# A two-layer hybrid encoder trunk: low weight halves of the mixers moved to GpSimd, index search dealt out in steps, reciprocals merged, feed-forward begun by two outputs

## The chip, the cores and the metric

The kernel runs on one core of one Trainium2 chip. The metric is device time in microseconds (us) of one execution; lower is better. The kernel before takes 1246.18 us (median of 3 runs, 1245.75 to 1247.45).

## The reference

A trunk of two layers over x of 512 frames by 1024 channels, float32. Each layer is RMSNorm, a mixer with residual, RMSNorm, and a gated feed-forward block with residual; a last RMSNorm ends it. Cut to what matters:

```python
# layer 0 mixer
qa, ka, va, qi, ki, wi, qb, kb, vb = _split(xn @ w_in, EVEN_SPLITS)
score = einsum('bqhs,bqh->bqs', relu(qi . ki), wi)      # index scores, masked by chunk
idx = top_k(score, 128)                                 # A: 8 heads, softmax over the 128 chosen keys
ya = softmax(qa . ka[idx] * scale) @ va[idx]
yb = softmax(qb . kb * scale + rel_bias) @ vb           # B: 8 heads, learned distance bias
y  = concat(ya, yb) @ w_out
# layer 1 mixer
F  = cumsum(log_sigmoid(fc + forget_b))                 # C: 8 heads, bias F[t] - F[s], causal
yc = softmax(qc . kc * scale + F[t] - F[s]) @ vc
yd = softmax_with_sink(qd . kd * scale, window) @ vd    # D: 8 heads on 2 key heads
y  = concat(yc, yd) @ w_out
# feed-forward, both layers (2816 wide)
g, u = split(conv3(xn @ w_up) + conv_b)
h = h + (silu(g) * u) @ w_down
```

## The kernel before

**Numbers in two halves.** TensorE works on float32r. Each weight tile of 128x1024 is loaded by SyncE into `raw` (2 buffers), ScalarE copies its rounded high half into `whi` (L136), and a subtraction makes the low half `wlo` (L138); both have 4 buffers. The activations are split likewise, and each product is three matmuls (`mm3`, L176 to L178: high by high, high by low, low by high). `Stream` (`W`) issues the 196 tiles in the order of `PLAN`; `W.ahead(2)` keeps two tiles prepared. The subtraction L138 runs on GpSimd for the keys `A1` and `kB` (8 tiles) and on VectorE for all others (188):

```python
eng = nc.gpsimd if key[0] in ('A1', 'kB') else nc.vector
```

**Order of the program.** First the index projection `i` (`tok_wide`), then values `vB` of the B heads in four pieces of 128 frames (`tok_group`; its four tiles are all used by each piece, 24 matmuls of 512 columns). Beside `vB` the index scores of the three later query blocks are made (`idx_scores`, into `wk1` to `wk3` of 256, 384 and 512 columns). Then q and k of the first pair of B heads (`chan_pair`; one tile gives one 128x512 output, 24 matmuls).

**Pairs and fill.** Attention goes by pairs of heads, B pairs 0 to 3, then A pairs. `weave(prev, cur, fill, n)` writes one pair's scores (`score`, L420) and softmax (`soft`), the pair before's transposes of probabilities (`turn`, L453, split by L183 on ScalarE and L184 on VectorE into `PTh`, `PTl`), its product with the values (`av`, L470 and L471) and its output (`store`), and between these n steps of `fill`. A step is one k of a projection, three matmuls. The queue of `fill` holds the other B pairs' q and k (48 steps), the projections A1, vA, A2 of the A heads (32 each, `tok_group`), the output projection oB (32) and oA. `FILL_B` and `FILL_A` say how many steps each weave takes; layer 1 has the same with `FILL_C` and `FILL_D`.

**Softmax.** `soft` adds the bias and takes the row extreme (L439, VectorE), takes the exponential with its sum (L441, ScalarE), a reciprocal of the sum (L442, VectorE, 128x1 for each of four query blocks) and scales the row (L443, GpSimd). `store` ends with the split of the pair's output `yT` into halves (L183 ScalarE, L184 VectorE).

**Index search.** The A heads keep 128 of the admissible keys. `topk(i)` finds them by 16 rounds of the eight largest (`max`, L664) and their replacement by a low number (`match_replace`, L665), then makes a bias of the result (L666, L667); it is written after the four B pairs, for i = 1, 2, 3. The framework's scheduler orders each engine's instructions by readiness, so these 48 rounds do not stand where they are written; they may go to VectorE as soon as the scores are there. Each engine then runs its own list strictly in order.

**Layer 1.** C heads take a row of F, spread over the partitions by a matmul with a selecting matrix `sel` that VectorE makes for each call (`forget_row`, L921, 12 calls). The D heads run in four units of 128 frames, whose probabilities GpSimd scales (L1064).

**Feed-forward.** For each of 22 j an output g and an output u are computed (`up`, 24 matmuls each), scaled by the norm's factors `R`, convolved and multiplied (`conv`); then the down projection. `R` comes from `token_roots` (L239) and `roots` (L249) after the first g.

Of the kernel before, what the change touches and what calls it, by code (L numbers as in the profile page):

```python
# [10 lines left out]
F32 = mybir.dt.float32  # L11
F32R = mybir.dt.float32r
# [64 lines left out]
FILL_B = (8, 20, 21, 22, 22)  # L77
FILL_A = (23, 30, 16, 14, 11)
# [8 lines left out]
def trunk(ctx, tc, a, out):  # L87
# [30 lines left out]
    class Stream:  # L118
# [4 lines left out]
        def issue(self):  # L123
            key = PLAN[self.pos]
            self.pos += 1
            if key[0] == "i":
                src, w = a["w_i"][key[1]], 2 * NI
            elif key[0] == "d":
                src, w = a["w_d"][key[1]], 2 * ND
            else:  # L130
                src, w = a["w"][WIDE_AT[key]], 1024
            raw = wp.tile([128, 1024], F32, name="raw", tag="raw", bufs=2)
            nc.sync.dma_start(raw[:, :w], src)
            hi = wp.tile([128, 1024], F32R, name="whi", tag="whi")
            lo = wp.tile([128, 1024], F32R, name="wlo", tag="wlo")
            nc.scalar.activation(hi[:, :w], raw[:, :w], AF.Copy)  # L136
            eng = nc.gpsimd if key[0] in ('A1', 'kB') else nc.vector
            eng.tensor_tensor(lo[:, :w], raw[:, :w], hi[:, :w].bitcast(F32), OP.subtract)  # L138
            self.ready[key] = (hi, lo)
# [119 lines left out]
    class Fill:  # L259
# [7 lines left out]
        def step(self, n):  # L267
            while n > 0 and self.q:
                try:
                    next(self.q[0])  # L270
                    n -= 1
                except StopIteration:
                    self.q.pop(0)
# [4 lines left out]

    def run(gen):
        for _ in gen:  # L280
            pass
# [111 lines left out]
    class Pair:  # L393
# [42 lines left out]
        def soft(self, e, rows):  # L436
            for i in rows:
                L, nm, sm = self.L[e][i], self.nm[e][:, i:i + 1], self.sm[e][:, i:i + 1]
# [3 lines left out]
                nc.vector.reciprocal(sm, sm)  # L442
                nc.gpsimd.tensor_scalar(L, L, sm, 1.0, op0=OP.mult, op1=OP.mult)  # L443
# [29 lines left out]
        def store(self, e):  # L473
# [7 lines left out]
            if e == 1:  # L481
                y = job["pair"]["y"] = self.mp.tile([128, 2, 512], F32R, name="yT", tag="yT",
                                                    bufs=5 if self.ybufs == 2 else 4)
                hilo(y[:, 0], y[:, 1], Y)
# [93 lines left out]
    with ExitStack() as st:  # L578
# [70 lines left out]

        VB = hp.tile([128, NT, 8, 2, HD], F32R, name="VB", tag="h")  # L650
# [8 lines left out]

        def topk(i):  # L660
            wk = work[i]
            for r in range(TOPK // 8):
                m8 = smp.tile([128, 8], F32, name="m8", tag="m8")
                nc.vector.max(m8, wk)  # L664
                nc.vector.match_replace(wk, m8, wk, -3e38)  # L665
            nc.vector.tensor_scalar(wk, wk, -2e38, BIG, op0=OP.is_gt, op1=OP.mult)  # L666
            nc.gpsimd.memset(wk[0:64, 128 * i + 64:128 * i + 128], BIG)  # L667
# [50 lines left out]
        nb = {hh: bias_b(hh)() for hh in range(2)}  # L718
        fill.step(FILL_B[0])

# [12 lines left out]
        for i in (1, 2, 3):  # L733
            topk(i)
# [17 lines left out]
    def ffn(layer, after):  # L752
        with ExitStack() as st:
# [20 lines left out]

            for j in range(NFF):
                tmp = sp.tile([128, 2, SEQ], F32, name="scr", tag="scr")
                g = up(("g", layer, j))
                if j == 0:
                    token_roots()
                    roots()  # L780
                conv(g, j, tmp[:, 0])
                nc.scalar.activation(tmp[:, 0], tmp[:, 0], AF.Silu)
                u = up(("u", layer, j))
# [61 lines left out]
    with ExitStack() as st:  # L845
# [72 lines left out]

        def forget_row(hh, w):
            sel = mp.tile([128, 128], F32R, name="sel", tag="PSh", bufs=1)  # L920
            nc.vector.tensor_tensor(sel, ident[:, hh:hh + 1].to_broadcast([128, 128]),  # L921
                                    ident[:, 32 + hh:33 + hh].to_broadcast([128, 128]), OP.add)
            pb = bank("s")
            nc.tensor.matmul(pb[:, :w], sel, FTh[:, :w], start=True, stop=True)
            return pb
# [294 lines left out]
```

## Time and profile before

| what | us |
|---|---|
| median of 3 runs | 1246.18 |
| profiled execution | 1248.47 |
| span of its instructions (first to last) | 1246.6 |
| PE busy (5908 matmuls) | 1211.3 |
| DVE busy | 826.8 |
| ACT busy | 592.6 |
| POOL busy | 198.4 |
| layer 0 mixer, about | 0 to 301 |
| layer 0 feed-forward, about | 301 to 656 |
| layer 1 mixer, about | 656 to 878 |
| layer 1 feed-forward and end | 878 to 1246.6 |

PE is TensorE, DVE VectorE, ACT ScalarE, POOL GpSimd, SP SyncE (it issues the loads). Busy shares are averages over stages that differ. A busy PE is not a PE at its peak, since matmuls overlap; the number of matmuls that start in a stretch says more than its busy time. A wait is put down to the releaser that came last.

### The profile page before, as it was taken

What the parts mean: (1) busy time and instruction counts of PE and PEld (TensorE: products, weight loads), DVE (VectorE), ACT (ScalarE), POOL (GpSimd) and SP (SyncE); (2) the same over time, 40 slices, a digit from 0 to 9 for tenths busy, and PEclk for the clock granted to TensorE, in tenths of its full rate; (3) what the DMA queues carried; (4) which work ended last, traced back from release to release, by engine and by line L of the source; (5) the groups of instructions that cost most, each with busy time, mean ns of one, the idle gap of its engine ahead of it and who ended that gap; (6) DMA issues with size and microseconds to landing.
All of it is one profiled execution on the core that took longest, in us unless ns stands there. A gap on an engine that the chain in (4) does not pass through costs nothing.

```text
span 1246.6 us, 15944 instructions
## 1 busy us (share of the span) xinstructions
PE 1211.3 (97%) x5908; PEld 996.3 (80%) x5908; DVE 826.8 (66%) x1528; ACT 592.6 (48%) x1008; POOL 198.4 (16%) x275
## 2 busy tenths in 40 slices
PE   8997999999999999999999999999999999999997
PEld 8776788787888888888888877777888888888886
DVE  7999867867777777742325466897777777772222
ACT  6444465656444444432224577785544444442221
POOL 3465322212000000000002254322000000000000
PEclk9998999999999999999999999999999999999999
DMA  6232124312333333333322321122233233223321
GB/s 215 82 105 68 35 68 135 103 50 88 102 101 96 91 100 102 92 95 101 101 64 90 102 68 35 35 76 75 90 102 98 90 100 102 92 95 101 101 68 68
DMA packets 35373, 111.71 MB, mean 90 GB/s; under 512 B 4192, under 2 KB 6624, under 8 KB 35296
## 3 DMA queue, kind: packets, MB, share of 16 engines
q1 hardware_dynamic: 35296, 110.70, 28.5%
q8 instruction: 46, 0.75, 0.3%
q14 instruction: 31, 0.25, 0.1%
HBM read 108.59 MB, written 2.10 MB: 89 GB/s over the span
## 4 chain that ended last, share of the span: by engine, by line
PE 78%; DVE 11%; ACT 5%; issue 3%; DMA 2%; POOL 1%; POOLq 0%; SPq 0%; DVEq 0%; ACTq 0%
PE acc L176 17%; PE acc L177 17%; PE acc L178 17%; PE s L176 7%; PE s L178 7%; PE s L177 7%; DVE wlo L138 2%; DVE wk L665 2%; DVE m L664 2%; PE tp L453 2%; ACT whi L136 1%; ACT P L441 1%; DMA raw<-in_w 1%; DVE xT L231 1%; DVE P L439 1%
## 5 line engine op out<-in xcount | busy, mean ns | idle before, releaser
L138 DVE TENSOR_TENSOR wlo<-raw,whi 128x1024 fp32r<-128x1024 f32 (+2 forms) x188 | 237.1, 1261 | 158.4 <-ACT whi L136 156.1
L136 ACT ACTIVATE whi<-raw 128x1024 fp32r<-128x1024 f32 (+2 forms) x196 | 204.6, 1044 | 210.8 <-PE acc L177 139.4
L176 PE MATMUL acc<-xT,whi 128*128 128x512 f32 x480 | 189.4, 395 | 1.0 <-DVE os L546 0.6
L178 PE MATMUL acc<-xT,wlo 128*128 128x512 f32 x480 | 187.7, 391 | 0.0
L177 PE MATMUL acc<-xT,whi 128*128 128x512 f32 x480 | 187.7, 391 | 0.0
L213 POOL TENSOR_TENSOR scr<-scr,os 128x512 f32<-128x512 f32 x24 | 34.1, 1421 | 730.5 <-ACT os L211 730.5
L176 PE MATMUL acc<-act,whi 128*128 128x512 f32 (+1 forms) x374 | 140.9, 377 | 0.0
L178 PE MATMUL acc<-act,wlo 128*128 128x512 f32 (+1 forms) x374 | 140.9, 377 | 0.0
L177 PE MATMUL acc<-act,whi 128*128 128x512 f32 (+1 forms) x374 | 140.9, 377 | 0.0
L176 PE MATMUL s<-xT,whi 128*128 128x512 f32 x352 | 137.6, 391 | 0.0
L178 PE MATMUL s<-xT,wlo 128*128 128x512 f32 x352 | 137.5, 391 | 0.0
L177 PE MATMUL s<-xT,whi 128*128 128x512 f32 x352 | 137.0, 389 | 0.0
L176 PEld LDWEIGHTS acc<-xT,whi 128*128 128x128 f32 x480 | 90.7, 189 | 20.9 <-issue 1.9
L178 PEld LDWEIGHTS acc<-xT,wlo 128*128 128x128 f32 x480 | 90.6, 189 | 19.1
L177 PEld LDWEIGHTS acc<-xT,whi 128*128 128x128 f32 x480 | 90.6, 189 | 18.0
L176 PE MATMUL acc<-whi,xT 128*128 128x512 f32 (+2 forms) x208 | 84.1, 406 | 2.1 <-ACT whi L136 1.9
L761 DVE TENSOR_TENSOR ov<-s,R 128x512 f32<-128x512 f32 x44 | 30.4, 692 | 79.6 <-PE s L178 79.6
L183 ACT ACTIVATE act<-scr 128x512 fp32r<-128x512 f32 x44 | 27.8, 631 | 115.8 <-DVE scr L785 115.8
L177 PE MATMUL acc<-wlo,xT 128*128 128x512 f32 (+2 forms) x208 | 80.7, 389 | 1.2 <-DVE wlo L138 1.1
L178 PE MATMUL acc<-whi,xT 128*128 128x512 f32 (+2 forms) x208 | 81.0, 390 | 0.1
L177 PEld LDWEIGHTS acc<-act,whi 128*128 128x128 f32 x374 | 70.4, 188 | 13.0
L178 PEld LDWEIGHTS acc<-act,wlo 128*128 128x128 f32 x374 | 70.4, 188 | 12.9
(250 smaller groups left out, 2235.3 us busy)
## 6 DMA issues: line engine op xcount, KB each, us to landing
raw<-in_w SPq DMA_DIRECT2D x188, 512.0 KB, 3.5
h<-in_x SPq DMA_DIRECT2D x16, 256.0 KB, 4.9
T<-in_relb SPq DMA_DIRECT2D x8, 256.0 KB, 3.0
raw<-in_w_i SPq DMA_DIRECT2D x4, 324.0 KB, 4.1
raw<-in_w_d SPq DMA_DIRECT2D x4, 264.0 KB, 2.7
out_y<-h SPq DMA_DIRECT2D x4, 256.0 KB, 2.2
out_y<-h SPq DMA_DIRECT2D x2, 384.0 KB, 2.4
ropeC<-in_ropeC SPq DMA_DIRECT2D x2, 256.0 KB, 4.0
```

What stands on the lines that cost most here:

```text
L136: nc.scalar.activation(hi[:, :w], raw[:, :w], AF.Copy)
L138: eng.tensor_tensor(lo[:, :w], raw[:, :w], hi[:, :w].bitcast(F32), OP.subtract)
L176: nc.tensor.matmul(o, lh, rh, start=start, stop=False)
L177: nc.tensor.matmul(o, lh, rl, start=False, stop=False)
L178: nc.tensor.matmul(o, ll, rh, start=False, stop=stop)
L183: nc.scalar.activation(dh, src, AF.Copy)
L213: eng.tensor_tensor(ss, ss, sq, OP.add)
L231: nc.vector.scalar_tensor_tensor(xT[1][:, c, :], H["h"][:, c, :], g, xT[0][:, c, :].bitcast(F32), op0=OP.mult, op1=OP.subtract)
L453: nc.tensor.transpose(pt[:, off:off + 128], self.L[e][i][:, j * 128:(j + 1) * 128], ident)
L664: nc.vector.max(m8, wk)
L665: nc.vector.match_replace(wk, m8, wk, -3e38)
L761: nc.vector.tensor_tensor(v, o, R, OP.mult)
```

## The change

Six edits. (1) `wlo` is made on GpSimd for every tile of the two mixers but `i` and `d`: 56 tiles, 48 more than before; VectorE keeps the feed-forward's, `i` and `d`. (2) The low half of a pair's output `yT` is made on GpSimd (12 of them). (3) In `soft` the reciprocals of the blocks 2, 0 and 3 are one instruction of 128x3 instead of three of 128x1. (4) `topk` becomes a generator of 17 steps; a queue `aside` takes one step at every second (during vB and the first q and k) or every third (during the B pairs) step of projections, and its `max` and `match_replace` are held to the program's order; `FILL_B` and `FILL_A` are other numbers, so that A1 and vA end with the B pairs. (5) The first g and u of a feed-forward block are computed with six of eight k each first, then the last two of each, and `token_roots` follows both. (6) `forget_row` gives the matmul one column of a small table `pick`, broadcast, and `sel` goes.

```diff
-FILL_B = (8, 20, 21, 22, 22)
-FILL_A = (23, 30, 16, 14, 11)
+FILL_B = (8, 26, 26, 26, 26)
+FILL_A = (18, 20, 14, 12, 11)
@@ Stream.issue
-            eng = nc.gpsimd if key[0] in ('A1', 'kB') else nc.vector
+            eng = nc.vector if key[0] in ("i", "d", "g", "u", "w") else nc.gpsimd
@@ Fill.step, run: after each step
+                    aside.tick()
+    class Aside:
+        def tick(self):
+            self.n += 1
+            if self.q and self.n % self.every == 0:
+                self.pop()
...
+    aside = Aside(2)
@@ Pair.soft
+            at = {1: 3, 2: 0, 0: 1, 3: 2}
             for i in rows:
...
-                nc.vector.reciprocal(sm, sm)
-                nc.gpsimd.tensor_scalar(L, L, sm, 1.0, op0=OP.mult, op1=OP.mult)
+            both = sms[:, at[rows[0]]:at[rows[-1]] + 1]
+            nc.vector.reciprocal(both, both)
+            for i in rows:
+                L = self.L[e][i]
+                nc.gpsimd.tensor_scalar(L, L, sms[:, at[i]:at[i] + 1], 1.0, op0=OP.mult, op1=OP.mult)
@@ Pair.store
-                hilo(y[:, 0], y[:, 1], Y)
+                nc.scalar.activation(y[:, 0], Y, AF.Copy)
+                nc.gpsimd.tensor_tensor(y[:, 1], Y, y[:, 0].bitcast(F32), OP.subtract)
@@ topk(i): now ahead of vB, and queued behind idx_scores
             for r in range(TOPK // 8):
                 m8 = smp.tile([128, 8], F32, name="m8", tag="m8")
-                nc.vector.max(m8, wk)
-                nc.vector.match_replace(wk, m8, wk, -3e38)
+                tc.keep_in_program_order(nc.vector.max(m8, wk))
+                tc.keep_in_program_order(nc.vector.match_replace(wk, m8, wk, -3e38))
+                yield
...
                 idx_scores(vb - 1)
+                aside.q.append(topk(vb - 1))
...
+        aside.every = 3
         fill.step(FILL_B[0])
...
-        for i in (1, 2, 3):
-            topk(i)
+        aside.drain()
@@ ffn
+            def first_two():
+                W.ahead(2)
+                os_ = bank("acc"), bank("s")
+                gens = [chan_mm(o, W.get((x, layer, 0), 128)) for x, o in zip("gu", os_)]
+                for gen in gens:
+                    for _ in range(KD - 2):
+                        next(gen)
+                for gen in gens:
+                    run(gen)
+                return os_
@@ forget_row
-            sel = mp.tile([128, 128], F32R, name="sel", tag="PSh", bufs=1)
-            nc.vector.tensor_tensor(sel, ident[:, hh:hh + 1].to_broadcast([128, 128]),
-                                    ident[:, 32 + hh:33 + hh].to_broadcast([128, 128]), OP.add)
-            nc.tensor.matmul(pb[:, :w], sel, FTh[:, :w], start=True, stop=True)
+            nc.tensor.matmul(pb[:, :w], pick[:, hh:hh + 1].to_broadcast([128, 128]), FTh[:, :w],
+                             start=True, stop=True)
```

**Place 1, VectorE, the end of B pair 0's weave.** The list of VectorE up to `PTl`, the low half of the first transposed probabilities of pair 0, which the scores of pair 1 wait for (they need its PSUM bank). `wk_545` and `wk_557` are the second block's scores, `wk_611` the third's, `os` is the evacuation of a q or k output. Before:

```order
L546 SCALAR_TENSOR_TENSOR os<-acc,R 128x512
L664 MAX m_1793<-wk_545 128x8
L665 MATCH_REPLACE wk_545<-m_1793,wk_545 128x384
L664 MAX m_1796<-wk_545 128x8
L665 MATCH_REPLACE wk_545<-m_1796,wk_545 128x384
L664 MAX m_1799<-wk_545 128x8
L664 MAX m_1804<-wk_611 128x8
L184 TENSOR_TENSOR PTl<-tp,PTh 128x512
L439 ISA P_956,nm<-tp,T 128x256
```

and now:

```order
L682 MAX m_991<-wk_557 128x8
L574 SCALAR_TENSOR_TENSOR os<-acc,R 128x512
L683 MATCH_REPLACE wk_557<-m_991,wk_557 128x384
L574 SCALAR_TENSOR_TENSOR os<-acc,R 128x512
L682 MAX m_1015<-wk_557 128x8
L683 MATCH_REPLACE wk_557<-m_1015,wk_557 128x384
L184 TENSOR_TENSOR PTl<-tp,PTh 128x512
L463 ISA P_1062,nm<-tp,T 128x256
```

Six search instructions stood between the last evacuation and `PTl`, the last of them of the third block; now two stand there, and six of the second block's 16 rounds come later.

**Place 2, GpSimd, the start of the program.** `T` is the distance bias, `ropeC` and `ropeS` the rotary tables, scaled here, `scr_305` the rotated index vector of the first 128 frames. Before:

```order
L224 TENSOR_TENSOR scr<-scr 128x1024 x2
L673 TENSOR_SCALAR T<-T 128x512
L674 MEMSET T 64x64
L673 TENSOR_SCALAR T<-T 128x512
L674 MEMSET T 64x64
L257 TENSOR_SCALAR ropeC<-ropeC,rs 128x128
L343 TENSOR_TENSOR scr_305<-scr 128x320
```

and now:

```order
L224 TENSOR_TENSOR scr<-scr 128x1024 x2
L138 TENSOR_TENSOR wlo<-raw,whi 128x1024
L703 TENSOR_SCALAR T<-T 128x512
L138 TENSOR_TENSOR wlo<-raw,whi 128x1024
L704 MEMSET T 64x64
L703 TENSOR_SCALAR T<-T 128x512
L704 MEMSET T 64x64
L257 TENSOR_SCALAR ropeC<-ropeC,rs 128x128
L138 TENSOR_TENSOR wlo<-raw,whi 128x1024
L365 TENSOR_TENSOR scr_305<-scr 128x320
```

Three of vB's four low halves now stand ahead of the first index vector in GpSimd's list; the fourth comes behind the second.

**Place 3, GpSimd, the D units of layer 1.** `P` and `PP` are the units' probabilities being scaled, `wlo` the tiles of oC and oD. Before:

```order
L1064 TENSOR_SCALAR PP<-PP,sm 128x256 x5
L343 TENSOR_TENSOR scr_7325<-scr 128x512
L1064 TENSOR_SCALAR PP<-PP,sm 128x256
L1064 TENSOR_SCALAR P<-P,sm 128x256 x6
L1064 TENSOR_SCALAR PP<-PP,sm 128x256 x6
```

and now:

```order
L1109 TENSOR_SCALAR PP<-PP,sm 128x256 x5
L365 TENSOR_TENSOR scr_7255<-scr 128x512
L1109 TENSOR_SCALAR PP<-PP,sm 128x256
L138 TENSOR_TENSOR wlo<-raw,whi 128x1024 x3
L1109 TENSOR_SCALAR P<-P,sm 128x256 x6
L138 TENSOR_TENSOR wlo<-raw,whi 128x1024
L1109 TENSOR_SCALAR PP<-PP,sm 128x256 x6
```

Three low halves now stand between the second unit's probabilities and the third's.

## Rows read from the trace of the kernel before

**Rows 1.** The page's first part and PE's row of its second part.

```profile
PE 1211.3 (97%) x5908; PEld 996.3 (80%) x5908; DVE 826.8 (66%) x1528; ACT 592.6 (48%) x1008; POOL 198.4 (16%) x275
...
PE   8997999999999999999999999999999999999997
```

**Rows 2.** Stretches: from:to, us, busy (and instructions) by engine, clock granted, DMA.

```profile
core 0: us, PE busy (x) PEld busy (x) DVE busy (x) ACT busy (x) POOL busy (x), PEclk, DMA share, GB/s
21.00:41.10 20.10, 19.54 (x96) 15.10 (x94) 18.93 (x55) 9.52 (x20) 12.08 (x19) 1.00 0.46 155
73.10:91.30 18.20, 17.04 (x90) 13.56 (x90) 17.62 (x57) 9.93 (x22) 12.34 (x17) 1.00 0.29 79
91.30:121.10 29.80, 24.85 (x124) 20.26 (x123) 28.49 (x79) 13.87 (x31) 16.36 (x18) 0.89 0.27 88
121.10:147.90 26.80, 24.03 (x138) 19.55 (x139) 24.35 (x65) 11.67 (x30) 12.73 (x19) 1.00 0.14 40
147.90:172.60 24.70, 24.00 (x143) 19.89 (x141) 20.65 (x50) 16.57 (x37) 6.82 (x10) 1.00 0.27 86
172.60:197.50 24.90, 24.62 (x138) 20.31 (x138) 16.48 (x40) 15.64 (x33) 4.26 (x8) 1.00 0.28 86
278.00:301.00 23.00, 21.30 (x86) 16.77 (x85) 18.98 (x22) 13.70 (x21) 9.29 (x6) 0.93 0.30 96
350.00:375.00 25.00, 25.00 (x112) 20.71 (x111) 17.43 (x22) 11.97 (x15) 0.00 (x0) 1.00 0.33 103
787.00:837.00 50.00, 48.05 (x279) 37.13 (x279) 46.45 (x159) 41.51 (x124) 15.20 (x26) 1.00 0.16 54
```

**Rows 3.** What PE waited for: us in total, times, longest us.

```profile
PE tp L420 <- DVE PTl L184: 7.8, 4, 4.9
...
PE acc L177 <- DVE wlo L138: 1.1, 2, 0.7
...
PE s L924 <- DVE sel L921: 0.5, 3, 0.2
```

**Rows 4.** Timeline, DVE and PE near 98: start, us, instruction, idle before.

```profile
97.42 0.67 DVE L184 TENSOR_TENSOR PTl<-tp,PTh 128x512 fp32r<-128x512 f32 x1
...
98.15 0.58 PE L420 MATMUL tp<-qk 64*128 64x256 f32 x1 [4.90 <-DVE PTl L184]
```

**Rows 5.** Groups by shape on DVE, 70 to 175: busy us, mean ns, idle before.

```profile
L664 DVE MAX8 m<-wk 128x8 f32<-128x512 f32 x16 | 11.1, 691 | 0.3
L665 DVE MATCH_REPLACE8 wk<-m,wk 128x512 f32<-128x512 f32 x16 | 10.8, 675 | 0.0
...
L138 DVE TENSOR_TENSOR wlo<-raw,whi 128x1024 fp32r<-128x1024 f32 x5 | 7.0, 1404 | 0.0
...
L442 DVE RECIPROCAL sm<-sm 128x1 f32<-128x1 f32 x33 | 5.0, 156 | 2.7 <-ACT P L441 2.5
```

**Rows 6.** Groups by shape on POOL, the whole span.

```profile
L138 POOL TENSOR_TENSOR wlo<-raw,whi 128x1024 fp32r<-128x1024 f32 x8 | 19.8, 2473 | 7.7 <-ACT whi L136 7.6
...
L443 POOL TENSOR_SCALAR P<-P,sm 128x256 f32<-128x256 f32 x24 | 11.6, 483 | 53.7 <-DVE sm L442 53.7
```

**Rows 7.** Timeline of DVE and POOL between 7 and 20.

```profile
7.19 0.83 DVE L138 TENSOR_TENSOR wlo<-raw,whi 128x648 fp32r<-128x648 f32 x1 [1.75 <-ACT whi L136]
...
16.15 2.78 POOL L224 TENSOR_TENSOR scr<-scr 128x1024 f32<-128x1024 f32 x1 [1.49 <-ACT scr L219]
...
16.60 3.02 DVE L138 TENSOR_TENSOR wlo<-raw,whi 128x648 fp32r<-128x648 f32 x1
```

**Rows 8.** Chain of waits, 155 to 163: start, us, what.

```profile
155.82 3.48 DMA raw<-in_w
...
159.32 1.06 ACT whi L136
...
161.25 1.67 DVE wlo L138
```

**Rows 9.** Timeline at the start: the first vB tile, and the last index vector.

```profile
19.93 1.04 ACT L136 ACTIVATE whi<-raw 128x1024 fp32r<-128x1024 f32 x1
...
40.23 0.87 POOL L343 TENSOR_TENSOR scr<-scr 128x320 f32<-128x320 f32 x1
```

**Rows 10.** Groups by shape on DVE, 787 to 837.

```profile
L138 DVE TENSOR_TENSOR wlo<-raw,whi 128x1024 fp32r<-128x1024 f32 x6 | 8.1, 1349 | 0.5 <-ACT whi L136 0.5
```

More of the change, by code (lines that the diff above doesn't have):

```diff
@@ L277, in run, with __init__, pop, drain @@
                 self.step(1)
+    class Aside:
+        def __init__(self, every):
+            self.q, self.every, self.n = [], every, 0
+        def tick(self):
+            self.n += 1
+            if self.q and self.n % self.every == 0:
+                self.pop()
+        def pop(self):
+            try:
+                next(self.q[0])
+            except StopIteration:
+                self.q.pop(0)
+        def drain(self):
+            while self.q:
+                self.pop()
+    aside = Aside(2)
     def run(gen):
         for _ in gen:
-            pass
+            aside.tick()
     def tok_group(name, ncol, evac):
@@ L436, in soft @@
         def soft(self, e, rows):
+            at = {1: 3, 2: 0, 0: 1, 3: 2}
+            nms, sms = self.nm[e], self.sm[e]
             for i in rows:
-                L, nm, sm = self.L[e][i], self.nm[e][:, i:i + 1], self.sm[e][:, i:i + 1]
+                L, nm, sm = self.L[e][i], nms[:, at[i]:at[i] + 1], sms[:, at[i]:at[i] + 1]
                 nc.vector.tensor_tensor_reduce(out=L, in0=self.s[e][i], in1=self.job["bias"][e][i], scale=1.0,
@@ L648, in idx_scores, with topk @@
             nc.gpsimd.memset(wk[0:64, w - 64:w], -BIG)
+        def topk(i):
+            wk = work[i]
+            for r in range(TOPK // 8):
+                m8 = smp.tile([128, 8], F32, name="m8", tag="m8")
+                tc.keep_in_program_order(nc.vector.max(m8, wk))
+                tc.keep_in_program_order(nc.vector.match_replace(wk, m8, wk, -3e38))
+                yield
+            nc.vector.tensor_scalar(wk, wk, -2e38, BIG, op0=OP.is_gt, op1=OP.mult)
+            nc.gpsimd.memset(wk[0:64, 128 * i + 64:128 * i + 128], BIG)
         VB = hp.tile([128, NT, 8, 2, HD], F32R, name="VB", tag="h")
@@ L658, in trunk @@
                 idx_scores(vb - 1)
[L660 to L663, printed above, removed]
-                nc.vector.max(m8, wk)
-                nc.vector.match_replace(wk, m8, wk, -3e38)
-            nc.vector.tensor_scalar(wk, wk, -2e38, BIG, op0=OP.is_gt, op1=OP.mult)
-            nc.gpsimd.memset(wk[0:64, 128 * i + 64:128 * i + 128], BIG)
+                aside.q.append(topk(vb - 1))
         def bias_b(hh):
@@ L773, in up @@
                 return o
+            def first_two():
[8 more added lines that the diff above has]
+                return os_
             for j in range(NFF):
                 tmp = sp.tile([128, 2, SEQ], F32, name="scr", tag="scr")
-                g = up(("g", layer, j))
                 if j == 0:
+                    g, u = first_two()
                     token_roots()
                     roots()
+                else:
+                    g = up(("g", layer, j))
                 conv(g, j, tmp[:, 0])
                 nc.scalar.activation(tmp[:, 0], tmp[:, 0], AF.Silu)
-                u = up(("u", layer, j))
+                if j > 0:
+                    u = up(("u", layer, j))
                 conv(u, NFF + j, tmp[:, 1])
@@ L917, in trunk @@
         pairs = [{} for _ in range(4)]
+        pick = mp.tile([128, 32], F32R, name="pick")[:, :8]
+        nc.vector.tensor_tensor(pick, ident[:, 0:8], ident[:, 32:40], OP.add)
         def forget_row(hh, w):
-            sel = mp.tile([128, 128], F32R, name="sel", tag="PSh", bufs=1)
-            nc.vector.tensor_tensor(sel, ident[:, hh:hh + 1].to_broadcast([128, 128]),
-                                    ident[:, 32 + hh:33 + hh].to_broadcast([128, 128]), OP.add)
             pb = bank("s")
-            nc.tensor.matmul(pb[:, :w], sel, FTh[:, :w], start=True, stop=True)
+            nc.tensor.matmul(pb[:, :w], pick[:, hh:hh + 1].to_broadcast([128, 128]), FTh[:, :w],
+                             start=True, stop=True)
             return pb
```

## Prediction

> **What bounds the kernel now.** I read the busy table and the slices first. PE is busy 97% of the span, and its row of slices is full but for the first slices and the last [rows 1]. In the feed-forward, 112 matmuls of 512 columns start in the 25 us from 350, at full clock [rows 2], so one costs 0.223 us and a fill step of three 0.67 us. Nothing the change does can shorten that; what it can gain is PE's lost time in the two mixers. So I cut layer 0's mixer at the starts of the pairs' scores [rows 2]. The stretches from 147.9 and 172.6 hold 22 and 23 fill steps (`FILL_B[4]`, `FILL_A[0]`), 14.7 and 15.4 us of the 24.7 and 24.9. What is left, 10.0 and 9.5 us, is a weave's own scores, transposes and products with their small gaps; I take 9.7 as the price of a weave. The stretch from 91.3 has 21 steps and should last 14.1 + 9.7 = 23.8 us; it lasts 29.8. The one from 121.1 has 22, should last 24.4, and lasts 26.8. DVE is busy 28.5 of the 29.8 us there, against 16.5 of 24.9 where the search is over. The wait list says who is late: PE's scores wait 7.8 us in four places for `PTl` [rows 3], the longest 4.90 us [rows 4], because in DVE's list search rounds stand in front of `PTl` (place 1). In that stretch the granted clock is 0.89, that is, PE ran part of it at 1.2 instead of 2.4 GHz, after it had idled. So in layer 0's B pairs the bound is DVE's queue, and a few us later PE again.
>
> **The sum, part by part.** It is made against the profiled execution, 1248.47 us (span 1246.6 and 1.9 around it), which lies 2.3 us above the median 1246.18.
>
> *B pairs.* The four weaves took 99.5 us from 73.1 to 172.6 [rows 2] with 20 + 21 + 22 + 22 = 85 steps. They now take 104; the 19 added ones (12.7 us) leave the A pairs and what follows, so they cost nothing in all. At the old pace the stretch would last 112.2 us. At PE's pace it lasts 26 x 0.67 + 9.7 = 27.1 us for each of three weaves. The first has no pair before it and spent 18.2 - 20 x 0.67 = 4.8 us beside its steps, some 0.9 of them waiting; at 3.9 it lasts 21.3. Together 102.6, a gain of 9.6 us, if DVE keeps up. A search round of 512 columns costs 0.69 + 0.68 us and a short load [rows 5], say 1.4; a step of `aside` falls on every third of 26, so 8 or 9 rounds, 12 us, on top of the 16.5 us of a weave without search [rows 2], less two or three low halves of 1.4 [rows 5] and some of the 33 reciprocals of 0.16 us. That is about 25 us of DVE in 27.1: it fits, barely. For this I give back 1 us: **-8.6**, between -2 (DVE stays the bound in two weaves) and -11.
>
> *Reciprocals, `yT`.* Both come off DVE. The reciprocals merge 64 into 32 in layer 0 and 32 into 16 in layer 1. They are in the DVE budget above and nothing else waits for them; a merged one holds the scaling of block 2 until block 3's sum is there, about two exponentials later, and the pair's probabilities are needed half a weave later. 0.
>
> *vB's low halves.* POOL needs 2.47 us for one [rows 6] where DVE takes 1.23 to 1.40. At the start POOL is busy 12.1 of the 20.1 us between 21.0 and 41.1, when the last index vector is ready [rows 2, 9]. Four low halves of 2.47 add 9.9: 22.0 us of work from 21.0, when the first vB high half is done [rows 9], end at 43.0 instead of 41.1. DVE loses its four there, but its index chain goes through POOL. So **+2**, between 0 and +5 (PE also waits for the fourth tile in `vB`'s first pieces). Rows show besides that the two engines hold each other up here: a low half of 0.83 us on DVE took 3.02 us when POOL had begun a two-operand add 0.45 us earlier [rows 7].
>
> The Trainium skill, "SBUF — State Buffer", section "SBUF: two separate sides", names the rule: a DVE instruction with two SBUF inputs and a GpSimd instruction take a shared port pair as an exclusive lock, for the whole instruction. The trace agrees, by the 3.02 us above. By that rule DVE's second add of squares (L226) would stand behind the first low half on POOL for up to 2.4 us, and with it the norm's factors, so this term would be about +4.4 and the time 2.4 us more than I forecast; in the weaves it costs nothing, since there DVE's second operand is nearly always in PSUM.
>
> *vA and A2.* These follow a projection whose four tiles stay in use to its end. There are two `raw` buffers, so the third tile's load can start only when the first low half is done, and then come 3.48 us of load, 1.06 of high half and the low half [rows 8]. On POOL both low halves in that chain are 1.1 to 1.2 us longer, so it comes up to 2.4 us later. PE already waited 1.1 us in all for low halves [rows 3]. POOL's other work is small instructions of 0.48 us and up [rows 6] but in order. I take **+3** for the two, between 0 and +5. oB follows A2 in the same way, and its burst of four stands in front of the last rotation of A2: **+1**, between 0 and +4. In layer 1 vC follows `d` with time to spare, and qD follows tiles that come free one by one: 0.
>
> *D units.* From 787 to 837 DVE is busy 46.5 of 50 us and PE idle 1.95 [rows 2]; six low halves are 8.1 of DVE's [rows 10]. They go. But three of them, 7.4 us, now stand in front of a unit's probabilities on POOL (place 3). Net **-2**, between -4 and +4.
>
> *`sel`.* PE waited 0.5 us for it [rows 3]; the broadcast column costs PE the same one load. **-0.5**, between -2 and 0.
>
> *First two outputs.* In 278 to 301 PE loses 1.7 us idle and runs at clock 0.93 [rows 2], that is 1.6 us more, but the cause is the output projection's residual and norm on DVE and POOL, which stay. The later `token_roots` is covered by the second g and u, 48 matmuls or 10.7 us. If this cover were gone, PE would wait for a PSUM bank. 0, between -3 and +0.5.
>
> Sum: -8.6 + 2 + 3 + 1 - 2 - 0.5 = **-5.1 us**. From the profiled execution that is 1243.4; from the median, which I forecast against, **1241.0 us**.
>
> **The rivals.**
>
> *GpSimd's queue becomes the bound (slower).* POOL is in order; 48 low halves of 2.47 us are 119 us more on it. Wherever a low half or a scaled row stands behind another that waits for its load, PE waits too. With the upper ends of vB (5), vA and A2 (5), oB (4) and the units (4), 18 us, less 8.6 and 0.5, it is 9 us slower: 1255 us; with two thirds of these ends 1249. It decides from about 11 us of new waits. For it: rows 6 and the lists at places 2 and 3. Against: half of POOL's span in the B pairs is idle [rows 2], and kB and A1 were there already with 1.1 us of waits.
>
> *DVE stays late in the B pairs (no change).* My DVE budget is 25 of 27.1 us. If rounds pile up where rotations and transposed halves come too, the gain is 2 to 3 us, and the +6 of the other terms takes it up: 1246 to 1249 us.
>
> *The new waits are hidden (more gain).* If the scheduler's order gives POOL its tiles early enough, +6 becomes +1, the units give -4 and the B pairs -10: 1231 us. For it: POOL's idle share, and that PE's loss in both mixers is still larger than all I claim.
>
> *The change doesn't do what it says.* The lists show rounds and low halves moved; this I rule out, except for the first two outputs, where u's first matmuls already stood ahead of the output projection's last: counted as 0.
>
> **How the numbers follow.** Forecast 1241.0 (1237 to 1245): 0.42. More gain, around 1231: 0.26. No change, around 1247.5: 0.13. Slower, around 1252: 0.19. About 0.2%, 2.5 us, is what a measurement of this kernel can tell from no change. Below 1243.7 lie four fifths of the forecast's case, all of the gain and a fifth of the third: 0.63. Within: 0.17. Above 1248.7: 0.20. The range for 8 in 10 goes from **1229** to **1252**.
>
> **What would show it.** Right: PE's wait for `PTl` falls from 7.8 us to under 3; the granted clock is 1.00 through the B pairs; four weaves take about 103 us; DVE is busy some 25 of 27 us in the third weave; PE waits 1 to 2 us each at the starts of vA and A2 for `wlo` on POOL, and the index scores come 2 us later. Wrong: waits of PE for `wlo` or `P` on POOL that sum over 8 us; search rounds still in front of `PTl` in time; or the pairs taking more than 108 us.

## The result, and the profile after

The changed kernel takes **1266.22 us** (median of 4 runs, 1265.83 to 1267.31), against 1246.78 for the kernel before on the same chip: a ratio of 1.0158, 95% interval [1.014, 1.0176]. It is slower by some 20 us. The forecast was 1241.0, with 1229 to 1252 for 8 in 10; the time lies outside. The profiled execution spans 1264.8 us.

The first part of the page, PE's row of slices, and POOL's row of the costliest groups, of the changed kernel:

```profile
PE 1213.6 (96%) x5908; PEld 1000.2 (79%) x5908; DVE 769.8 (61%) x1409; ACT 591.1 (47%) x1008; POOL 315.8 (25%) x335
...
PE   8889999899999999999999999889999999999997
...
L138 POOL TENSOR_TENSOR wlo<-raw,whi 128x1024 fp32r<-128x1024 f32 x56 | 135.0, 2419 | 69.9 <-ACT whi L136 54.7
```

The matmuls are as many as before [rows 1] and DVE has lost 57 us of work, POOL has gained 117. Yet PE's second and third slices, the start of layer 0's mixer, and two in the middle of its right half, layer 1's units, are now less full (the fourth, where the scores waited for `PTl`, is fuller). With work added to an engine that was idle for 84% of the span, PE waits more.

The stretches of the changed kernel, cut at the starts of the pairs' scores as in [rows 2], and two of the D units:

```profile
core 0: us, PE busy (x) PEld busy (x) DVE busy (x) ACT busy (x) POOL busy (x), PEclk, DMA share, GB/s
21.00:41.10 20.10, 12.93 (x61) 9.67 (x61) 18.00 (x41) 6.81 (x13) 16.96 (x18) 0.99 0.41 130
41.10:50.00 8.90, 8.90 (x40) 7.10 (x38) 3.93 (x11) 2.57 (x7) 2.97 (x7) 0.84 0.15 55
85.10:106.10 21.00, 20.79 (x107) 17.02 (x107) 15.99 (x51) 12.45 (x25) 17.79 (x20) 1.00 0.39 122
106.10:131.00 24.90, 24.90 (x141) 20.96 (x140) 19.52 (x56) 12.72 (x29) 17.11 (x20) 1.00 0.32 89
131.00:160.60 29.60, 26.93 (x151) 21.86 (x150) 24.50 (x66) 15.03 (x34) 17.35 (x19) 1.00 0.19 64
160.60:188.10 27.50, 26.24 (x142) 21.19 (x142) 21.48 (x57) 14.86 (x34) 10.41 (x14) 1.00 0.09 29
...
830.00:840.00 10.00, 8.41 (x34) 6.32 (x32) 7.58 (x25) 5.96 (x20) 5.23 (x7) 0.83 0.16 52
850.00:860.00 10.00, 8.31 (x33) 6.56 (x33) 6.17 (x20) 6.11 (x14) 4.97 (x7) 0.83 0.16 53
```

Read it from the second row down. The four weaves of the B pairs run from 85.1 to 188.1, 103.0 us, at full clock: the part of the change that was to gain does what was forecast (102.6). But they begin at 85.1 instead of 73.1. In the 20.1 us from 21.0 PE starts 61 matmuls where it started 96 [rows 2], and after these waits it runs at a granted clock of 0.84, that is partly at 1.2 instead of 2.4 GHz. So 12 us are lost before the first pair. Layer 1's first scores start at 720.7 against 709.5, its down projection at 1131.8 against 1113.6: of the 18 us there, 7 are lost between these two, in layer 1's mixer, in whose units 34 and 33 matmuls start in two stretches of 10 us, at clock 0.83.

What PE waited for in the changed kernel, the largest entries and some small ones (waiter, released by: us in total, times, longest):

```profile
PE acc L177 <- POOL wlo L138: 7.3, 4, 3.8
PE acc L176 <- DVE h L368: 6.8, 5, 2.4
PE acc L176 <- DVE os L574: 3.5, 1, 3.5
...
PE acc L177 <- POOL yT L512: 2.4, 2, 2.0
PE tp L442 <- POOL qk L576: 2.2, 2, 2.0
...
PE acc L176 <- DVE sm L1101: 1.2, 1, 1.2
...
PE tp L442 <- DVE PTl L184: 0.3, 1, 0.3
```

The wait of the scores for `PTl`, 7.8 us before [rows 3], is down to 0.3. Waits for `wlo` on POOL have come, 7.3 us, but more are waits for DVE: 6.8 for the residual `h`, 3.5 for `os`. DVE has less to do than before and is late all the same. Its timeline says why; here with POOL's and PE's instructions beside it, at the start and in the units:

```profile
20.86 3.37 POOL L138 TENSOR_TENSOR wlo<-raw,whi 128x1024 fp32r<-128x1024 f32 x1 [2.65 <-ACT whi L136]
...
21.99 2.78 DVE L226 TENSOR_TENSOR scr<-scr 128x512 f32<-128x512 f32 x1
...
31.55 2.36 POOL L138 TENSOR_TENSOR wlo<-raw,whi 128x1024 fp32r<-128x1024 f32 x1
...
31.69 2.57 DVE L363 TENSOR_TENSOR scr<-ir,ropeC 128x320 f32<-128x320 f32 x1
...
36.06 0.85 POOL L365 TENSOR_TENSOR scr<-scr 128x320 f32<-128x320 f32 x1
...
37.41 2.38 POOL L138 TENSOR_TENSOR wlo<-raw,whi 128x1024 fp32r<-128x1024 f32 x1
...
39.85 0.50 PE L177 MATMUL acc<-wlo,xT 128*128 128x512 f32 x1 [3.78 <-POOL wlo L138]
...
830.80 2.42 POOL L138 TENSOR_TENSOR wlo<-raw,whi 128x1024 fp32r<-128x1024 f32 x1 [4.35 <-ACT es L1100]
...
830.87 2.37 DVE L1099 TENSOR_TENSOR es<-nm,sink 128x2 f32<-128x2 f32 x1
...
835.48 0.50 PE L176 MATMUL acc<-yT,whi 128*128 128x512 f32 x1 [1.59 <-DVE h L368]
```

Two mechanisms stand in these rows. **POOL's order:** vB's fourth low half, whose high half ACT finished at 33.0, starts at 37.41, because the rotations of two index vectors stand in front of it in POOL's list; PE waits 3.78 us for it. **Held-up DVE:** an addition of 128x2, two numbers a partition, takes 2.37 us, because POOL began a low half 0.07 us earlier. It ends within 0.02 us of POOL's instruction; the larger ones end a little after it. The residual's addition, which stands some instructions behind it in DVE's list, comes that much later, and PE, which needs the residual's PSUM bank, waits 1.59 us; the 10 us around it have a granted clock of 0.83. The second add of squares takes 2.78 us instead of 0.69, a rotation 2.57 instead of 0.48 to 0.49.

### The profile page after: what moved, and what is told of

Its sections match the earlier page's. It is cut to its first block, busy times and chain, and to the rows that moved or that the text cites. A ratio compares the mean times of both kernels' runs of the same rounds, so it can differ in the third digit from the quotient of the medians.

```text
span 1264.8 us, 15915 instructions
## 1 busy us (share of the span) xinstructions
PE 1213.6 (96%) x5908; PEld 1000.2 (79%) x5908; DVE 769.8 (61%) x1409; ACT 591.1 (47%) x1008; POOL 315.8 (25%) x335
## 4 chain that ended last, share of the span: by engine, by line
PE 74%; DVE 7%; POOL 5%; issue 5%; ACT 5%; DMA 3%; POOLq 0%; SPq 0%; DVEq 0%; ACTq 0%
PE acc L177 16%; PE acc L176 16%; PE acc L178 16%; PE s L177 7%; PE s L178 7%; PE s L176 7%; POOL wlo L138 3%; DMA raw<-in_w 2%; ACT whi L136 2%; PE tp L480 2%; PE tp L497 1%; PE s L442 1%; PE tp L498 1%; ACT P L465 1%; DVE PTl L184 1%
## 5 line engine op out<-in xcount | busy, mean ns | idle before, releaser
L138 DVE TENSOR_TENSOR wlo<-raw,whi 128x1024 fp32r<-128x1024 f32 (+2 forms) x140 | 172.6, 1233 | 144.0 <-ACT whi L136 141.4
L138 POOL TENSOR_TENSOR wlo<-raw,whi 128x1024 fp32r<-128x1024 f32 x56 | 135.0, 2419 | 69.9 <-ACT whi L136 54.7
L176 PE MATMUL acc<-whi,xT 128*128 128x512 f32 (+2 forms) x208 | 86.2, 414 | 1.3 <-ACT whi L136 1.1
L178 PE MATMUL acc<-whi,xT 128*128 128x512 f32 (+2 forms) x208 | 82.1, 395 | 1.0 <-DVE xT L231 1.0
L176 PEld LDWEIGHTS acc<-act,whi 128*128 128x128 f32 x374 | 70.4, 188 | 13.0
L177 PEld LDWEIGHTS acc<-act,whi 128*128 128x128 f32 x374 | 70.4, 188 | 12.7
```

Source lines behind the costliest of these rows:

```text
L176: nc.tensor.matmul(o, lh, rh, start=start, stop=False)
L177: nc.tensor.matmul(o, lh, rl, start=False, stop=False)
L178: nc.tensor.matmul(o, ll, rh, start=False, stop=stop)
```

## The experiments

The theory (L) is that the low halves on GpSimd cost the time, by both mechanisms. The rivals are that the dealt-out search does (S), or `yT` and the merged reciprocals (Y). All versions were timed in three rounds against the kernel before, whose median was 1245.3 to 1246.8 in the several sets. Costs below are differences of ratios, with 0.001 as 1.25 us; the expectations used medians, which gives up to 1.2 us more or less.

| version | median us | ratio to before, 95% interval |
|---|---|---|
| the change | 1266.22 | 1.0158 [1.014, 1.0176] |
| E1: mixers' low halves back on VectorE | 1236.26 | 0.9918 [0.9899, 0.9937] |
| E2: before, with the search and fill alone | 1239.46 | 0.9946 [0.9926, 0.9966] |
| E3: change, vB back | 1256.45 | 1.0082 [1.006, 1.0104] |
| E4: change, units' additions with one operand | 1257.51 | 1.0092 [1.0073, 1.0112] |
| E5: change, first two tiles of vB back | 1262.68 | 1.0135 [1.0113, 1.0157] |
| E6: E1 with E4's units | 1236.79 | 0.9928 [0.9907, 0.995] |
| E7: E6, layer 1's mixer on GpSimd | 1238.81 | 0.9947 [0.9927, 0.9968] |
| E8: E6, qB on GpSimd | 1241.46 | 0.9966 [0.9955, 0.9977] |
| E9: E1, vA, A2, oB, oA on GpSimd | 1242.56 | 0.9977 [0.9968, 0.9987] |
| E10: E1, vA on GpSimd | 1235.83 | 0.9918 [0.9903, 0.9933] |
| E11: E1, a search step at every second step | 1239.83 | 0.9956 [0.9941, 0.9971] |
| E12: E1, yT and reciprocals as before | 1235.80 | 0.9925 [0.9908, 0.9941] |

**E1, the low halves back.** `Stream.issue`:

```diff
-            eng = nc.vector if key[0] in ("i", "d", "g", "u", "w") else nc.gpsimd
+            eng = nc.gpsimd if key[0] in ("A1", "kB") else nc.vector
```

> The change with its first part undone: the low halves of the mixers' weights are made on VectorE again, except A1 and kB; everything else as changed. Theory L (the 48 low halves on GpSimd cost the time: they stand in line there, and while one runs VectorE's instructions with two operands in SBUF stand still): the waits of PE for wlo made on GpSimd, 7.3 us, fall under 2, the first scores start at about 74 us instead of 85.1, the feed-forward of layer 1 begins some 18 us earlier, and the time is 1239 to 1247 us. Rival S (the search rounds tied to projection steps cost it, since four of them stand in front of an evacuation that PE waits for, 3.5 us at 74): that wait stays at 2.5 us or more, and the time stays above 1255. Rival Y (yT's low half on GpSimd and the merged reciprocals): the time stays above 1258 and PE still waits over 2 us for yT.

Measured 1236.26, faster than both kernels and below the range expected. Edit 1 of the six therefore costs 0.0240, some 30 us, and the other five together gain about 10. Its first scores start at 71.2, before those of the kernel before; layer 1's down projection starts 30 us earlier than in the change, where 18 were expected. No wait for `wlo` on POOL is left in PE's list. Its waits of PE that answer to the change's:

```profile
PE acc L176 <- DVE h L368: 2.8, 3, 1.7
PE tp L442 <- DVE PTl L184: 2.7, 3, 1.2
...
PE acc L177 <- POOL yT L512: 1.0, 2, 0.6
```

The wait for `os` is not in the list: rivals S and Y are out as the main cause. The wait for `h`, 6.8 us in the change, is 2.8.

**E2, the search alone** (the new `FILL_B`, `FILL_A`, the queue `aside` and `topk` as a generator in the kernel before).

> The kernel before with the search dealt out in tied steps and the new FILL_B and FILL_A, and nothing else of the change. By theory L the search is worth what the pairs' starts show: in the change the four weaves of the B pairs last 103.0 us with 104 steps where the old pace would give 112; with the low halves on VectorE that is 2 or 3 more of 1.4 us in each weave, so DVE needs about 28 of 27 us: a gain of 2 to 8, 1239 to 1245 us. Rival S (the ties themselves cost): 1250 or more, with a wait of PE for os of over 2 us before the first scores.

Measured 1239.46, a gain of 0.0054 or 6.7 us: the search is worth what the pairs' starts said. E1 is 0.0028 below it, but the intervals overlap.

**E3, vB's four tiles back on VectorE** (`"vB"` added to the change's list of keys for VectorE).

> The change with the four low halves of vB alone back on VectorE. Theory L: of the 12.0 us by which the first scores start late (85.1 against 73.1), the wait for the third and fourth low half (1.7 and 3.8 us), the slow clock after them (0.83 from 40 to 50, 1.7 us) and the norm's factors held up by 2.1 us go: the first scores start at 75 to 78, and the time is 1256 to 1260. Rival S: the first scores start no earlier than 81, since rounds and evacuations set that stage, and the time is 1262 or more.

Measured 1256.45, a gain of 0.0076 or 9.5 us; the first scores start at 76.6. **E5** divides it: only `("vB", 0)` and `("vB", 1)` go back.

> The change with the first two of vB's four low halves on VectorE and the last two on GpSimd. It divides the 9.8 us that all four gave back (1266.2 to 1256.5). If VectorE's held-up instructions at the norm (the second add of squares, 2.78 us instead of 0.69, and the table of reciprocal roots, 1.79 instead of 0.69, both beside a low half) are the larger part, this gives 3 us or more: 1260 to 1263. If the place of the fourth low half in GpSimd's list is the larger part (behind the rotations of two index vectors, 3.8 us of waiting of PE and the slow clock after it), little comes back: 1263 to 1267, and PE still waits 3 us or more for wlo made on GpSimd.

Measured 1262.68: 2.9 us come back, with intervals that overlap. The time lies at the edge of the first range, but the wait of over 3 us is the sign of the second. In its timeline the second add of squares takes 0.69 again and the table of roots 0.90 (0.90 in the kernel before too, not the 0.69 of the expectation), and the norm's factors are in time; but PE's waits for the third and fourth tile are as they were:

```profile
32.23 0.50 PE L177 MATMUL acc<-wlo,xT 128*128 128x512 f32 x1 [1.68 <-POOL wlo L138]
...
38.08 0.73 PE L177 MATMUL acc<-wlo,xT 128*128 128x512 f32 x1 [3.72 <-POOL wlo L138]
```

So, by the medians, about a third of vB's cost is the norm held up by the first two low halves, the rest the last two tiles. How the rest divides between POOL's order and the rotations on DVE that the third low half held up (2.57 us at 29.95 here too), which feed that order, was not separated.

**E4, the units' additions with one operand.** POOL has the same work and the same low halves as in the change. Only the two small additions are written so that DVE reads one operand: the sink enters as ScalarE's bias, and `ss` holds both terms of the sum side by side. Cut to what matters; the tiles `ss` and `rc` are made in `begin`:

```diff
-                    nc.vector.tensor_tensor(es, self.nm[g][:, c], sink[:, ...], OP.add)
-                    nc.scalar.activation(es, es, AF.Exp)
-                    nc.vector.tensor_tensor(sm, sm, es, OP.add)
-                    nc.vector.reciprocal(sm, sm)
+                    for j in (2 * u, 2 * u + 1):
+                        nc.scalar.activation(self.es[g][:, j:j + 1], self.nm[g][:, j:j + 1], AF.Exp,
+                                             bias=sink[:, 4 * g + j:4 * g + j + 1])
+                    rc = self.rc[g][:, c]
+                    nc.vector.tensor_reduce(rc, self.ss[g][:, :, c].rearrange("p a b -> p b a"), ...)
+                    nc.vector.reciprocal(rc, rc)
```

> The change with the D units' two small additions on VectorE written so that neither reads two operands from SBUF: the sink is added by ScalarE as the bias of its exponential, and the sum is one reduction over a tile that holds both terms. The low halves stay on GpSimd, in the same order. Theory L in its strong form (an addition of 128x2 took 2.37 and 2.27 us instead of 0.15 because a low half of 2.4 ran on GpSimd, and the residual's addition behind it came late): PE's waits for h in the units (1.6 at 835 and 2.4 at 851) fall under 0.5 each, the clock there is 1.00, and the time falls by 3 to 7 us, 1259 to 1263. Rival O (only GpSimd's order counts, probabilities standing behind low halves): the waits stay and the time is within 1.5 us of the change's 1266.2.

Measured 1257.51, a gain of 0.0066 or 8.2 us, more than expected, from instructions that take 0.15 us each when nothing holds them. The groups by shape on DVE in the units, of the change (790 to 875; columns as in [rows 5]):

```profile
L1101 DVE TENSOR_TENSOR sm<-sm,es 128x2 f32<-128x2 f32 x16 | 6.3, 394 | 0.7 <-ACT es L1100 0.4
L1099 DVE TENSOR_TENSOR es<-nm,sink 128x2 f32<-128x2 f32 x16 | 5.6, 349 | 0.0
```

and of E4:

```profile
L1105 DVE TENSOR_REDUCE rc<-ss 128x2 f32<-128x4 f32 x16 | 2.5, 155 | 5.0 <-ACT ss L1102 4.8
```

The mean of 394 and 349 ns is that of many additions of 0.15 us and four of 1.05 to 2.37. The reduction, on the same values, stays at 155 ns, though eight of the 16 begin while a low half runs on POOL. E4's units run at clock 1.00, and PE's waits for `h` in them are gone; its largest wait there is 0.68 us, for `rc`.

E4 alone does not settle rival O, that only GpSimd's order counts there: the scheduler orders every list anew, and in E4's list of POOL the three low halves of place 3 no longer stand in a row but one by one between the scaled rows. What this gave, if anything, is part of the 8.2 us and was not separated. Against O speaks the change itself. None of PE's waits between 790 and 875 is for the units' `P` or `PP` on POOL, and the change's chain of waits, 826 to 838, runs through the held-up addition to the residual that PE waits for at 835.48:

```profile
830.96 2.28 DVE es L1099
...
834.82 0.61 DVE h L368
```

**E6** is the control: the same units where no low half runs on GpSimd beside them.

> The version with the mixers' low halves back on VectorE (1236.3 us) and, beside that, the D units' additions with one operand from SBUF. No low half runs on GpSimd beside the units then, so theory L expects little: GpSimd's scalings of 0.48 us are all that the additions can meet, 1233 to 1237 us. If instead the rewritten units were faster for another reason (fewer instructions on VectorE), the 8.7 us that they gave in the change would come again: 1227 to 1230.

Measured 1236.79 against 1236.26: nothing. The rewritten units gain only when there is something to hold them up. **E7** puts layer 1's low halves on GpSimd again, with these units.

> The same, but with the low halves of layer 1's mixer (vC, qC, kC, qD, oC, oD) on GpSimd; the units have their one-operand additions. If held-up additions in the units were all that the low halves cost in layer 1, this equals the version without them within 1.5 us. The starts of the pairs say otherwise: between the change and the version with the halves on VectorE, layer 1 lost 3 us before the first C pair and up to 4 at its start, where the low half of q and k stands behind weight tiles. By that it is 2 to 6 us slower than the same with the halves on VectorE.

Measured 0.0019 or 2.4 us above E6, at the low end of what was expected and with intervals that overlap; PE's wait for `qk` on POOL is in its list with 2.9 us, 2.3 the longest.

**E8, qB's low halves on GpSimd,** an attempt at a better version.

> The same, but with the three or four q tiles of the B pairs on GpSimd too (beside kB and A1), where VectorE is the bound: in the version with the halves on VectorE, the third stretch of pairs takes 34.1 us with VectorE busy 31.3 of them. Low halves there can come off VectorE without GpSimd being late, as half of GpSimd's span is free. If so, 1.4 us for each of two or three tiles comes off that stretch: 1230 to 1234 us. If qk's low halves on GpSimd then stand behind them, as at the first C pair, no gain: 1235 to 1239.

Measured 1241.46, 0.0038 or 4.7 us slower than E6, above both ranges expected. What was late was not `qk` but `os`, the wait that rival S had named. The lines of E8, DVE with POOL and PE:

```profile
57.57 5.21 POOL L138 TENSOR_TENSOR wlo<-raw,whi 128x1024 fp32r<-128x1024 f32 x2 [2.21 <-ACT whi L136]
...
58.01 5.32 DVE L675 SCALAR_TENSOR_TENSOR wk<-P,wi,wk 128x512 f32<-128x512 f32 x2 [1.51 <-ACT P L671]
...
67.06 0.68 DVE L574 SCALAR_TENSOR_TENSOR os<-acc,R 128x512 f32<-128x512 f32 x1
...
67.89 0.71 PE L176 MATMUL acc<-xT,whi 128*128 128x512 f32 x1 [3.29 <-DVE os L574]
```

and of E1, whose qB stays on VectorE:

```profile
59.28 1.60 DVE L675 SCALAR_TENSOR_TENSOR wk<-P,wi,wk 128x512 f32<-128x512 f32 x2
...
63.63 0.68 DVE L574 SCALAR_TENSOR_TENSOR os<-acc,R 128x512 f32<-128x512 f32 x1
```

Two index-score instructions of the fourth block take 5.32 us instead of 1.60, beside two low halves of 5.21. The four search rounds behind them, tied to the program's order, then stand in front of the evacuation `os`. In the change the same pair of rows is at 68.00 (5.31 us), and PE waits 3.5 us. The ties alone do not make the wait, since E1 has them too and PE does not wait for `os` there. That they turn a held-up DVE into a wait of PE is read from the lists; low halves on GpSimd without the ties were not run.

**E9, vA, A2, oB and oA on GpSimd.**

> The version with the mixers' low halves on VectorE (1236.3 us), with those of vA, A2, oB and oA on GpSimd beside kB and A1. The whole of the 48 low halves costs 30.0 us (1266.2 less 1236.3); so far vB gave 9.8 of it, held-up additions in the units 8.7, the q tiles of the B pairs 4.7 and the rest of layer 1 2.0. If the parts add up, 4.8 us are left for these sixteen tiles: 1241 us (1239 to 1243). By the prediction's terms for vA, A2 and oB (3 and 1 us) it is 1240. If they are hidden, 1235 to 1237, and what is missing lies in how the parts act on each other.

Measured 1242.56, inside the range of the parts that add up; by the ratios 0.0059 or 7.4 us above E1. These tiles wait for POOL in another way than the forecast had it. The chain of waits in the change, 186 to 198, at the start of A2:

```profile
186.17 2.38 POOL wlo L138
...
188.56 3.77 DMA raw<-in_w
...
192.35 1.06 ACT whi L136
...
195.34 0.59 ACT PTh L183
...
195.95 0.70 DVE PTl L184
...
196.69 0.50 PE tp L497
```

POOL's low half releases the `raw` buffer, the load starts 0.01 us later, and ACT, which has come to the high half in its list, stands 3.23 us for that load. Behind it are the exponentials and the transposed halves that PE wants. PE's wait is put down to `PTl` and `nm` on DVE; `wlo` is not waited for there at all (once elsewhere in E9, 1.2 us). ACT's waits for loads between 100 and 300 us, first of E1, then of E9:

```profile
ACT whi L136 <- DMA raw<-in_w: 5.8, 3, 3.9
...
ACT whi L136 <- DMA raw<-in_w: 11.5, 6, 3.5
```

They are 5.7 us longer in E9, where the kernel takes 7.4 us more. How much of this reaches PE was not separated.

**E10, vA alone on GpSimd.**

> The same version with vA's four low halves alone on GpSimd. They come in the stretch from 118.8 to 152.9, which takes 34.1 us with VectorE busy 31.2 of them, 5.2 for these four; GpSimd is busy 13.5 of it. If VectorE's load sets that stretch, 2 to 4 us come off: 1232 to 1235. If the third tile's chain (load, high half, low half) sets it, as was forecast for vA, nothing to 2 us more: 1236 to 1239.

Measured 1235.83, the same as E1, between the two ranges expected. By the pairs' starts the third weave falls from 34.1 to 29.3 us, and the fourth grows from 23.7 to 27.9: what the load of DVE gave, the next weave took back.

**E11, more rounds early** (the line `aside.every = 3` left out).

> The same version with a search step at every second projection step also during the B pairs, instead of every third. The first two weaves have VectorE idle for 4.7 of 21.4 and 5.4 of 26.2 us, the third for 2.9 of 34.1; with rounds taken there earlier, the third and fourth weave lose some 10 of their 16 rounds of 1.4 us. If VectorE's load in the third weave is the bound, 2 to 5 us come off: 1231 to 1235. If rounds in front of the transposed halves cost it again, PE's wait for PTl rises over 4 us and nothing is gained: 1236 to 1240.

Measured 1239.83, 0.0038 slower than E1. The wait of the change's aim is back, the largest of its list:

```profile
PE tp L442 <- DVE PTl L184: 6.0, 3, 4.3
```

**E12, yT and the reciprocals as before.**

> The same version with the reciprocals taken one by one again and the low half of yT on VectorE, that is, parts 2 and 3 of the change undone as well. They were costed at nothing. If that holds, 1235 to 1238 us. If they were the 3.2 us by which this version (1236.3) is below the one with the search alone (1239.5), 1238 to 1240; then the first two outputs and the broadcast column gave nothing.

Measured 1235.80, the same as E1 within the intervals: these two parts cost and gain nothing once the low halves are away. The waits for `yT` on POOL (2.4 us in the change, 1.0 in E1) come from the low halves in front of it.

**The sum of the parts.** vB 9.5, units 8.2, vA with A2, oB and oA 7.4, qB 4.7, the rest of layer 1 2.4: 32.2 us, against 30.0 for all at once. By the intervals of the table each part is uncertain by some 3 us (an estimate), so the two agree within that; whether the parts overlap can't be told.

## Why the prediction was wrong

The parts of the change other than the weights' low halves were forecast at -9.1 us and gave about -10. The 48 low halves were forecast at +2 + 3 + 1 - 2 = +4 us and cost 30. Two terms of that sum failed by mechanism, one was missing.

*B pairs, -8.6: right.* The four weaves last 103.0 us, forecast 102.6; the clock is 1.00 in all of them; the wait for `PTl` falls from 7.8 us to 0.3. That the sum agrees so closely is partly luck: the second weave lasts 24.9 and the third 29.6, where 27.1 was forecast for each. Besides, the bounds 147.9 and 172.6 of the forecast's stretches lie some 0.5 us behind the first scores there (147.42 and 171.98), so the four old weaves last 98.9 us and not 99.5, and the forecast gain is 0.6 us too large. In the third weave DVE is busy 24.5 us, forecast 25, though the weave lasts 29.6 with a wait for vA's low half and for `Y` in it. Alone this part gains 6.7 us (E2), with VectorE still making qB's and vA's low halves in these weaves.

*Reciprocals and `yT`, 0: right* (E12), save for `yT` behind low halves.

*vB's low halves, +2 (0 to +5): the first step that failed.* It measured +9.5 us. The first scores start 12.0 us later; with the four tiles back they start at 76.6, 8.5 us earlier. The sum set POOL's 22.0 us of work against its end at 43.0, as if only the last of it mattered. Within that list the fourth low half came after two index vectors, and PE waited for it from 36 on, not at the end. The order stood in the list at place 2; the step did not ask who waits for each entry. The other third is the held-up norm. There the rule weighed in the prediction, the Trainium skill's "SBUF — State Buffer", section "SBUF: two separate sides", said what came: the second add of squares was to be late by up to 2.4 us, and it took 2.78 us instead of 0.69, 2.1 more (E5 sets it right). The forecast left it out of its sum.

*Units, -2 (-4 to +4): the second step that failed, and the larger error.* They lost 8.2 us, by E4 and E6, to held-up additions and what these brought with them. The working counted DVE's 8.1 us of low halves as gained and looked for a loss only in POOL's order at place 3. The sentence "in the weaves it costs nothing, since there DVE's second operand is nearly always in PSUM" held for the weaves: among the pairs of layer 0 no VectorE instruction is stretched by over 0.6 us. It was not asked of the units, the rotations and the index scores, where both operands lie in SBUF. The trace of the kernel before had such a case, an index score that began 0.33 us after one of kB's low halves on POOL and took 2.62 us instead of 0.74:

```profile
60.55 2.62 DVE L647 SCALAR_TENSOR_TENSOR wk<-P,wi,wk 128x512 f32<-128x512 f32 x1
```

*No term for qB's tiles.* They were counted as DVE's gain in the budget of the weaves and never as a cost. They cost 4.7 us (E8), most of it through the index scores and `os` before the first pair, whose scores start at 75.1 instead of 71.5.

*vA, A2 and oB, +4 (0 to +9): inside the range, near twice its middle, and wrong in place.* It is 7.4 us with oA (E9), and nothing for vA alone (E10), to which part of the +3 was given. By the chain at A2 it comes through ACT's list and hardly through waits for `wlo`; of the change's 7.3 us of waits for `wlo`, 5.4 are vB's. The mark set for a failure, waits for `wlo` and `P` of over 8 us, does not show it: they are 7.3 and 0.7 us.

*Layer 1's vC and qD, 0:* 2.4 us for all of layer 1's tiles (E7), not told from nothing. *`sel` and the first two outputs, -0.5:* E12 against E2 holds these two alone, 0.9925 against 0.9946, a gain of up to 2.6 us with overlapping intervals; open.

*The rival.* GpSimd's queue as the bound was given 0.19 and 1249 to 1255 us. It came true in kind, with 1266.2 us well above its price, since a second mechanism stands beside it: over a quarter of the cost, the units alone, comes for the most part from held-up DVE instructions and not from POOL's order, and the index scores and the norm add to it. POOL's idle half in the B pairs, which was the argument against, told nothing of either.

## What to carry to other kernels

Before work goes to GpSimd, list for each place it will run which VectorE instructions there read two operands from SBUF, or are a `TENSOR_SCALAR`, and who waits behind them; here even an addition of 128x2 took as long as the subtraction of 128x1024 beside it. Then walk the in-order lists of POOL and of ACT entry by entry: a longer step on an idle engine frees a buffer later, and the engine that waits for the load holds everything behind it. If the work must be there, a form on VectorE that is not held up, as the reduction in E4, gives part of the loss back (8.2 us of 30 here). The better version here, 0.8% below the kernel before, keeps the search's new order and leaves the low halves where they were (E1, E10, E12).

## What the runs showed of the hardware

Which VectorE instruction is held up goes by its kind and operands, not by its size. Beside the low half at 74.77 the search rounds of the change go on at their usual pace; each of their instructions reads one operand, the replaced eight being loaded by an instruction of their own:

```profile
74.77 2.34 POOL L138 TENSOR_TENSOR wlo<-raw,whi 128x1024 fp32r<-128x1024 f32 x1 [1.25 <-ACT whi L136]
...
75.19 0.43 DVE L682 MAX8 m<-wk 128x8 f32<-128x256 f32 x1
...
75.73 0.41 DVE L683 MATCH_REPLACE8 wk<-m,wk 128x256 f32<-128x256 f32 x1
```

Additions, rotations and index scores with both operands in SBUF waited for the end of POOL's instruction (2.37, 2.57 and 5.32 us for two), and so did all others of that form that began beside a low half in the 14 traces. Subtractions with one operand in PSUM did not: `PTl` began beside a low half over a hundred times and never took more than 0.69 us. The reduction in E4 did not either (155 ns over 16). But one operand is no safeguard by itself. A `TENSOR_SCALAR`, which reads one tile and two numbers a partition, was held too; in E5 one of 128x64, beside a low half of POOL that began at 35.67, took 2.33 us instead of 0.30:

```profile
35.75 2.33 DVE L628 TENSOR_SCALAR ir<-ir,mv,rstd 128x64 f32<-128x64 f32 x1
```

What the waits cost beyond themselves is the clock: after 3.78 us without matmuls the stretch from 41.1 was granted 0.84, and the units' two stretches 0.83, between the levels of 1.2 and 2.4 GHz. In the units the change's waits for `h` and `sm` are 5.2 us and E4's for `h` and `rc` 1.3, so some 4 us went; two stretches of 10 us at 0.83 are 3.4 us more at full clock (an estimate), and 8.2 came back. In E4 the clock there is 1.00.
